# One weight load in five expert groups is cut by rows into transfers of 112, 8 and 8 rows

## The chip, the cores and the metric

The kernel runs on one core of a Trainium2 chip. A core has a matrix engine (TensorE, PE in the profile, with its weight loads as PEld), a vector engine (DVE), a scalar engine (ACT), GpSimd (POOL) and a sync engine (SP). SP issues nearly all transfers between the main memory and the on-chip memory; sixteen DMA engines carry them out. The on-chip memory has 128 rows (partitions). The metric is the device time of one execution in microseconds (us). Before the change it is 1357.66 us, the median of three runs from 1356.56 to 1358.91 us.

## What is computed

The reference is one decoder block on 256 tokens of width 2048: a norm, a token mixer (retention heads beside a state-space mixer, one input and one output projection), a norm, and a mixture of 32 experts in 4 groups with two experts chosen per token, then a final norm. The part that the change touches is the mixture of experts:

```
for grp in range(N_EXPERT_GROUPS):
    sl = slice(grp * EXPERTS_PER_GROUP, (grp + 1) * EXPERTS_PER_GROUP)
    a = jnp.einsum('td,edf->tef', ht, w_gate[sl])
    u = jnp.einsum('td,edf->tef', ht, w_up[sl])
    act = (jax.nn.silu(a.astype(f32)) * u.astype(f32) * comb[:, grp, :, None]).astype(h.dtype)
    out = out + jnp.einsum('tef,efd->td', act, w_down[sl]).astype(f32)
```

All three weight tensors of all 32 experts are read once: 32 x 3 x 2048 x 512 numbers of 4 bytes, 403 MB.

## The kernel before

The mixer comes first. Then the experts run in eight groups of four (`NG`, `GE`). The tokens that chose an expert of the group are gathered by matmuls with a 0/1 matrix (`gather`, tile `xg`, 32 places per expert). Three stages follow: the gate product (`project` into `pgate`), the up product (`project` into `pup`), and, after the product of the two, the down products with the scatter back to the tokens (`finish`, `back`).

The weights of a group lie in the main memory as 24 blocks of 128 rows by 4096 numbers, which are 16 KB a row and 2 MB a block. A block holds two tiles, each of which serves one step of 32-row matmuls for the four experts: blocks 0 to 7 are gate weights, 8 to 15 up weights, 16 to 23 down weights. The generator `stream` (line 762) takes the next buffer (`slot`, in the fixed order of `turns`, from rings of two to three buffers each and two halves of a larger tile named `twin`), issues one transfer on SP for the block (line 768), and hands out its two halves. In the last group alone the last two blocks go in two halves by columns.

What sets the order around the change is the program's own order and eight completion counters, which the transfers use in turn. A transfer waits on SP until the transfer eight places before it has landed, and until the matmuls that read the old content of its buffer are done. So at most eight transfers are under way. PE waits for a block's counter before the first matmul that reads it. `group` (line 1017) calls `stream` for one group. The last stage of the last group is followed by the final norm and the stores of the output.

Of the kernel before, what the change touches and what calls it, by code (L numbers as in the profile page):

```python
# [18 lines left out]
P = 128  # L19
# [14 lines left out]
NG = NE // GE  # L34
# [9 lines left out]
RING_A = 2  # L44
RINGS = {"a": RING_A, "b": 3, "e": 3, "n": 1}
SCRATCH = 256
PAD = 1.5e38


# [100 lines left out]
def block_kernel(tc, I, out):  # L150
    nc = tc.nc
    act, dve, pe, pool, sp = nc.scalar, nc.vector, nc.tensor, nc.gpsimd, nc.sync
# [6 lines left out]
    def stt(o, a, s, b, op0, op1, **k):  # L159
        dve.scalar_tensor_tensor(o, a, s, b, op0=op0, op1=op1, **k)  # L160

    def ts(o, a, s1, s2, op0, op1=None):
        if op1 is None:
            dve.tensor_scalar(o, a, s1, None, op0=op0)  # L164
        else:
            dve.tensor_scalar(o, a, s1, s2, op0=op0, op1=op1)
# [585 lines left out]
    def slot(n, name="wt"):  # L752
        if n in "cd":
            return twin("cd".index(n), 4).rearrange("p a b c -> p (a b) c")
        return rings[n].tile([P, 8, 512], F32, tag="w", name=name)
# [3 lines left out]
        sp.dma_start(w, src)  # L759
        return w  # L760

    def stream(src, n, single=0):

        for i in range(n // 2):
            w = slot(next(turns))
            s = src(i)
            for p in ((0, 4), (4, 8)) if i >= n // 2 - single else ((0, 8),):
                sp.dma_start(w[:, slice(*p)], s[:, slice(*p)])
            yield w[:, :4]
            yield w[:, 4:]  # L770

# [64 lines left out]
    lg = sm.tile([P, NT, 40], F32, name="lg")  # L836
    pool.memset(lg[:, :, :4], -PAD)
    mask = cp.tile([P, NT, NE], BF16, name="mask")
# [4 lines left out]
    def small(name, n):  # L843
        return sm.tile([P, NT, n], F32, name=name)


    gv, ev = small("gv", 15), small("ev", 14)
    pool.memset(gv[:, :, :7], -2 * PAD)
    pool.memset(ev[:, :, :6], -2 * PAD)
    mg, me = gv[:, :, 7:8], ev[:, :, 6:7]  # L850
# [4 lines left out]
    def b48(a):  # L855
        return a.unsqueeze(2).to_broadcast([P, 4, 8])
# [4 lines left out]
    def g48(a):  # L861
        return a.rearrange("p (g e) -> p g e", g=4)
# [11 lines left out]
    def route(t):  # L874
# [3 lines left out]
        dve.max(gv[:, t, 7:], lg[:, t, :8])  # L878
        dve.match_replace(gm[:, t], gv[:, t, :8], lg[:, t, :8], PAD)
        stt(mle[:, t], b48(gm[:, t, 4:]), PAD, g48(lg[:, t, 8:]), EQ, MUL)  # L880
        ts(g4[:, t], gm[:, t, 4:], PAD, None, EQ)
        dve.tensor_reduce(le[:, t], mle[:, t].rearrange("p g e -> p e g"), axis=AX, op=ADD)
# [132 lines left out]
        return nxt  # L1015

    def group(g):
        return stream(lambda i: I["wexp"][g, i], 48, 2 if g == NG - 1 else 0)


    xg = xgp.tile([P, KT, P], F32, name="xg")
    pgate = pbank("pg")
    ws = group(0)
    for k0, n in ((0, 1), (1, 1), *((k, 2) for k in range(2, KT, 2))):
        gather_part(xg, k0, n, (0, 1) if n == 1 else (1, 0))
# [81 lines left out]
    for g in range(NG):  # L1107
        if g:
            pgate = pbank("pg")
            ws = group(g)  # L1110
            project(pgate, xg, ((k, next(ws)) for k in range(KT)))
        if g + 1 < NG:
            e = slice(GE * g + GE, GE * g + 2 * GE)
            xg, swt = finish(xg, swt, pgate, ws, lambda: gather(posm[:, :, e], comb[:, :, e]), first=(g == 0))
        else:
            finish(xg, swt, pgate, ws, None, final_part)
# [5 lines left out]
    with tc.For_i(0, rounds, 1):  # L1122
        ts(posm, posm, -float(CAP), None, ADD)
        with tc.For_i(0, NG, 1) as gi:
            gd = bass.ds(gi, 1)
            ws = stream(lambda i: I["wexp"][gd, i].rearrange("a p e f -> p (a e) f"), 48)
            xg, swt = gather(posm[:, :, :GE], comb[:, :, :GE])
            pgate = pbank("pg")
            project(pgate, xg, ((k, next(ws)) for k in range(KT)))
            finish(xg, swt, pgate, ws)  # L1130
            for a in (posm, comb):
                tmp = ep.tile([P, NT, NE], F32, name="rot")
                dve.tensor_copy(tmp[:, :, :NE - GE], a[:, :, GE:])
                dve.tensor_copy(tmp[:, :, NE - GE:], a[:, :, :GE])
                dve.tensor_copy(a, tmp)
        for c0, n in ((0, 512), (512, 512), (1024, 512), (1536, P), (1664, P), (1792, P), (1920, P)):
            final_part(c0, n)
        final_norm()
# [19 lines left out]
```

## Time and profile before

| quantity | value |
|---|---|
| median of three runs | 1357.66 us (1356.56 to 1358.91) |
| profiled execution, its own time | 1354.11 us |
| its span, first to last instruction | 1352.3 us |
| mean granted share of PE's clock | 0.902 |
| PE busy | 1048.4 us (78%) |
| DVE busy | 401.3 us (30%) |
| ACT busy | 275.2 us (20%) |
| moved by the transfers | 487.03 MB, mean 360 GB/s |
| share of transfers in the chain that ended last | 61% |

The profile comes from one execution. Its span is cut into 40 slices of 33.8 us for the busy digits. The chain that ended last is followed back from the last instruction, at each step to what released it; a row "DMA" in it is the time from a transfer's issue to its landing. The DMA share is the mean busy share of the sixteen DMA engines in a stretch: at 0.5, half of their time is busy, be it half of the engines or all of them half of the time.

### The profile page before, as it was taken

Reading aid. Unit: us, or ns where it says so; the run is one execution under the profiler, and the core shown is the slowest. Engines: PE = TensorE matmul, PEld = TensorE weight load, DVE = VectorE, ACT = ScalarE, POOL = GpSimd, SP = SyncE. Lnnn points to the kernel's source line nnn. Section 1 sums busy time; section 2 is a strip of 40 time slices with the busy share of each in tenths; the row PEclk is TensorE's granted clock in tenths of the full one; section 3 lists DMA queues with packets and bytes.
Section 4 is the critical chain, followed back from the end, with each engine's and each line's share of the span. In section 5 each row is a group of like instructions: output and inputs, shape, how many; then the busy total and the mean of one; then the engine's idle time right before and its main releaser. Section 6 shows DMA issues by size and latency. Waiting matters only on the chain.

```text
span 1352.3 us, 17251 instructions
## 1 busy us (share of the span) xinstructions
PE 1048.4 (78%) x7319; PEld 597.4 (44%) x7319; DVE 401.3 (30%) x843; ACT 275.2 (20%) x512; POOL 6.7 (0%) x20
## 2 busy tenths in 40 slices
PE   9999999999999985587658557656855766585654
PEld 6999999888786441143114103211311321131112
DVE  6659878665556130021002002100200210020013
ACT  6655544555444000000000000000000000000003
POOL 0000000000000000000000000000000000000000
PEclk9999999999999998888789878977887997897888
DMA  9554555585976999999999999999999999999995
GB/s 376 213 179 145 206 209 203 187 324 188 404 274 227 383 426 427 428 426 425 427 428 429 426 426 427 427 427 427 426 427 427 429 426 426 427 428 427 426 426 217
DMA packets 38003, 487.03 MB, mean 360 GB/s; under 512 B 4481, under 2 KB 5153, under 8 KB 8353
## 3 DMA queue, kind: packets, MB, share of 16 engines
q1 hardware_dynamic: 37634, 485.58, 87.1%
q8 instruction: 59, 0.97, 0.3%
q10 hardware_dynamic: 288, 0.31, 0.1%
q14 instruction: 22, 0.18, 0.0%
HBM read 483.75 MB, written 2.11 MB: 359 GB/s over the span
## 4 chain that ended last, share of the span: by engine, by line
DMA 61%; PE 37%; DVE 0%; issue 0%; ACT 0%; SPq 0%; POOLq 0%; POOL 0%; DVEq 0%; ACTq 0%
DMA wt<-wexp 40%; DMA twin<-wexp 20%; PE pb L353 4%; PE pb L351 4%; PE pb L352 4%; PE pf L363 3%; PE pf L364 3%; PE pf L365 3%; PE po L723 2%; PE po L721 2%; PE po L722 2%; PE py L967 1%; PE pu L967 1%; PE pxg L941 1%; PE pg L967 1%; PE psc L998 1%
## 5 line engine op out<-in xcount | busy, mean ns | idle before, releaser
L967 PE MATMUL pu<-wt,xg 128*32 128x512 f32 x864 | 142.6, 789 | 97.6 <-DMA wt<-wexp 97.6
L967 PE MATMUL pg<-wt,xg 128*32 128x512 f32 x832 | 133.3, 769 | 87.8 <-DMA wt<-wexp 87.8
L157 DVE TENSOR_TENSOR wl<-w,wh 128x512 fp32r<-128x512 f32 x224 | 151.3, 689 | 72.6 <-ACT wh L285 71.8
L285 ACT ACTIVATE wh<-w 128x512 fp32r<-128x512 f32 x224 | 139.0, 630 | 138.2 <-PE pb L352 71.7
L157 DVE TENSOR_TENSOR sg<-sg,pu 128x512 f32<-128x512 f32 x8 | 5.5, 689 | 535.2 <-PE pu L967 534.1
L967 PE MATMUL py<-wt,at 128*32 128x128 f32 (+1 forms) x1456 | 115.7, 427 | 17.9 <-DMA wt<-wexp 17.7
L967 PEld LDWEIGHTS pu<-wt,xg 128*32 128x32 f32 x864 | 28.6, 128 | 208.3 <-DMA wt<-wexp 157.8
L967 PEld LDWEIGHTS pg<-wt,xg 128*32 128x32 f32 x832 | 25.3, 125 | 182.4 <-DMA wt<-wexp 137.8
L157 DVE TENSOR_TENSOR acc<-acc,psc 128x128 f32<-128x128 f32 (+1 forms) x98 | 43.3, 459 | 171.0 <-PE psc L998 170.9
L998 PE MATMUL psc<-y,swt 128*128 128x128 f32 (+1 forms) x224 | 72.7, 448 | 26.1 <-ACT y L995 25.5
L967 PEld LDWEIGHTS py<-wt,at 128*32 128x32 f32 x1456 | 42.5, 111 | 79.5 <-issue 37.8
L995 ACT ACTIVATE y<-py 128x128 f32<-128x128 f32 (+1 forms) x56 | 23.2, 415 | 233.9 <-PE py L967 233.8
L952 ACT ACTIVATE swt<-psw 128x256 f32<-128x256 f32 x8 | 3.1, 387 | 324.8 <-PE psw L950 324.8
L998 PEld LDWEIGHTS psc<-y,swt 128*128 128x128 f32 x224 | 33.8, 194 | 69.9 <-ACT y L995 57.7
L351 PE MATMUL pb<-xh,wh 128*128 128x256 f32 x224 | 64.3, 287 | 0.0
L941 PEld LDWEIGHTS pxg<-selr,h 128*128 128x128 f32 x512 | 61.2, 199 | 6.5 <-issue 5.9
L984 ACT ACTIVATE sg<-pg 128x512 f32<-128x512 f32 x8 | 4.8, 597 | 290.4 <-PE pg L967 290.4
L351 PE MATMUL pb<-twin,wh 128*128 128x256 f32 x224 | 63.8, 285 | 0.0
L941 PE MATMUL pxg<-selr,h 128*128 128x128 f32 x512 | 63.1, 284 | 0.6 <-DVE selr L164 0.6
L353 PE MATMUL pb<-xh,wl 128*128 128x256 f32 x224 | 63.4, 283 | 0.0
L352 PE MATMUL pb<-twin,wh 128*128 128x256 f32 x224 | 63.4, 283 | 0.0
L353 PE MATMUL pb<-twin,wl 128*128 128x256 f32 x224 | 63.4, 284 | 0.0
(256 smaller groups left out, 1449.2 us busy)
## 6 DMA issues: line engine op xcount, KB each, us to landing
wt<-wexp SPq DMA_DIRECT2D x156, 2048.0 KB, 39.1
twin<-wexp SPq DMA_DIRECT2D x34, 2048.0 KB, 39.1
w<-win SPq DMA_DIRECT2D x24, 2048.0 KB, 8.1
wt<-wout SPq DMA_DIRECT2D x6, 2048.0 KB, 12.4
w<-wout SPq DMA_DIRECT2D x2, 2048.0 KB, 7.9
wt<-wexp SPq DMA_DIRECT2D x4, 1024.0 KB, 31.9
w<-win SPq DMA_DIRECT2D x3, 1024.0 KB, 11.3
twin<-x SPq DMA_DIRECT2D x1, 2048.0 KB, 14.9
```

Of the source, the lines that this page charges most:

```text
L157: dve.tensor_tensor(o, a, b, op=op)
L285: act.activation(wh, w[:, i:i + n], AF.Copy)
L351: pe.matmul(o, wh[:, s], xh(k), start=(k == 0 and c % 2 == 0), stop=False, skip_group_check=True)
L352: pe.matmul(o, wh[:, s], xl(k), start=False, stop=False, skip_group_check=True)
L353: pe.matmul(o, wl[:, s], xh(k), start=False, stop=(k == KT - 1), skip_group_check=True)
L363: pe.matmul(ps[t], lh(k)[:, s], wh, start=(k == 0), stop=False)
L364: pe.matmul(ps[t], lh(k)[:, s], wl, start=False, stop=False)
L365: pe.matmul(ps[t], ll(k)[:, s], wh, start=False, stop=(k == KT - 1))
L721: pe.matmul(ps[t], yh[:, s], wh, start=(k == 0), stop=False)
L941: pe.matmul(px[:, i], h[:, t, (k0 + i) * P:(k0 + i + 1) * P], selr[:, t], start=(i == 0 and x == 0), stop=(x == NT - 1), skip_group_check= ...
L967: pe.matmul(ps[s], lhsT[:, s], w(j), **k)
L998: pe.matmul(px, swt[:, t * P:(t + 1) * P], y, start=True, stop=True)
```

## The change

In each of the groups 1 to 5, block 12 of the 24 (an up block) is moved in three transfers instead of one: rows 0 to 111, rows 112 to 119, and rows 120 to 127, all 4096 numbers wide. The bytes, the buffers and the order of the blocks stay. Nothing else is changed. The groups 0, 6 and 7 are loaded as before.

```
+APART_AT = 12
...
-    def stream(src, n, single=0):
+    def stream(src, n, single=0, apart=()):
 
         for i in range(n // 2):
             w = slot(next(turns))
             s = src(i)
             for p in ((0, 4), (4, 8)) if i >= n // 2 - single else ((0, 8),):
-                sp.dma_start(w[:, slice(*p)], s[:, slice(*p)])
+                for r in ((0, 112), (112, 120), (120, 128)) if i in apart else ((0, P),):
+                    sp.dma_start(w[slice(*r), slice(*p)], s[slice(*r), slice(*p)])
             yield w[:, :4]
             yield w[:, 4:]
...
     def group(g):
-        return stream(lambda i: I["wexp"][g, i], 48, 2 if g == NG - 1 else 0)
+        return stream(lambda i: I["wexp"][g, i], 48, 2 if g == NG - 1 else 0, (APART_AT,) if 0 < g < 6 else ())
```

The first place is SP's queue in group 1, around block 12. The names DMAHW0 to DMAHW7 are the eight completion counters, and PE_49 is PE's; the size is rows by numbers. Before:

```order
L768 DMA wt<-wexp 128x4096 [waits DMAHW0_49,PE_49]
L768 DMA wt<-wexp 128x4096 [waits DMAHW1_49,PE_49]
L768 DMA wt<-wexp 128x4096 [waits DMAHW2_49,PE_49]
L768 DMA twin_5187<-wexp 128x4096 [waits DMAHW3_49,PE_49]
L768 DMA wt<-wexp 128x4096 [waits DMAHW4_49,PE_49]
```

And with the change:

```order
L771 DMA wt<-wexp 128x4096 [waits DMAHW0_49,PE_49]
L771 DMA wt<-wexp 128x4096 [waits DMAHW1_49,PE_49]
L771 DMA wt<-wexp 112x4096 [waits DMAHW2_49,PE_49]
L771 DMA wt<-wexp 8x4096 [waits DMAHW3_49]
L771 DMA wt<-wexp 8x4096 [waits DMAHW4_49]
L771 DMA twin_5189<-wexp 128x4096 [waits DMAHW5_49,PE_49]
L771 DMA wt<-wexp 128x4096 [waits DMAHW6_49,PE_49]
```

The block takes three counters instead of one, so the blocks behind it use a counter two places further on; for the same counter, a block behind waits for a transfer that is now closer to it by two small ones.

The second place is PE's queue in the up product of group 1, where the same block is read. Before:

```order
L967 MATMUL pu<-wt,xg 32x512 [waits DMAHW1_49]
L967 MATMUL pu<-wt,xg 32x512 x7
L967 MATMUL pu<-wt,xg 32x512 [waits DMAHW2_49]
L967 MATMUL pu<-wt,xg 32x512 x7
L967 MATMUL pu<-twin_5187,xg 32x512 [waits DMAHW3_49]
```

And with the change:

```order
L970 MATMUL pu<-wt,xg 32x512 [waits DMAHW1_49]
L970 MATMUL pu<-wt,xg 32x512 x7
L970 MATMUL pu<-wt,xg 32x512 [waits DMAHW4_49,DMAHW3_49,DMAHW2_49]
L970 MATMUL pu<-wt,xg 32x512 x7
L970 MATMUL pu<-twin_5189,xg 32x512 [waits DMAHW5_49]
```

PE's instructions and their order are the same; the first matmul on the block waits for three landings instead of one.

## Rows read from the trace of the kernel before

**Rows 1.** The page's 40 slices: busy tenths of the DMA engines, and GB/s.
```profile
DMA  9554555585976999999999999999999999999995
GB/s 376 213 179 145 206 209 203 187 324 188 404 274 227 383 426 427 428 426 425 427 428 429 426 426 427 427 427 427 426 427 427 429 426 426 427 428 427 426 426 217
```
**Rows 2.** The chain that ended last, by engine.
```profile
DMA 61%; PE 37%; DVE 0%; issue 0%; ACT 0%; SPq 0%; POOLq 0%; POOL 0%; DVEq 0%; ACTq 0%
```
**Rows 3.** The same chain in order of time: start us, us, what.
```profile
496.37 39.15 DMA wt<-wexp
535.59 39.16 DMA twin<-wexp
574.80 39.14 DMA wt<-wexp
614.02 40.68 DMA wt<-wexp
...
811.60 40.63 DMA wt<-wexp
...
1009.15 40.66 DMA wt<-wexp
...
1216.47 40.64 DMA wt<-wexp
...
1295.09 33.21 DMA wt<-wexp
1328.43 0.81 PE py L967 x18
```
**Rows 4.** SP's own waits: us in total, times, longest us.
```profile
SPq L768 <- DMA wt<-wexp: 570.4, 133, 6.0
SPq L768 <- DMA twin<-wexp: 138.1, 31, 6.0
```
**Rows 5.** Busy time, 700 to 800: PE, PEld, DVE, ACT, POOL, clock, DMA share, GB/s.
```profile
700.00:800.00 100.00, 67.95 (x522) 26.20 (x514) 12.29 (x28) 3.89 (x9) 0.00 (x0) 0.86 1.01 427
```
**Rows 6.** Transfers from 500 to 1324 us, by queue and by issue.
```profile
q1 hardware_dynamic: 24206, 351.14, 100.4%
q8 instruction: 31, 0.51, 0.3%
...
wt<-wexp SPq DMA_DIRECT2D x131, 2048.0 KB, 39.1
```
**Rows 7.** End of the weights: stretch, us, PE's clock, DMA share, GB/s.
```profile
1326.00:1327.00 1.00, 1.00 0.97 401
1327.00:1328.00 1.00, 1.00 0.73 303
1328.00:1329.00 1.00, 1.00 0.61 254
1329.00:1330.00 1.00, 1.00 0.57 238
1330.00:1331.00 1.00, 1.00 0.51 213
1331.00:1332.00 1.00, 1.00 0.49 205
1332.00:1333.00 1.00, 1.00 0.49 205
1333.00:1334.00 1.00, 1.00 0.33 123
1334.00:1335.00 1.00, 1.00 0.20 82
1335.00:1336.00 1.00, 1.00 0.04 16
```
**Rows 8.** The issues of the weight transfers on SP: duration in ns min/median/max.
```profile
L768 SPq DMA_DIRECT2D wt<-wexp x160: 327/328/1184, 335.3 to 1306.2; - x160
```

More of the change, by code (lines that the diff above doesn't have):

```diff
@@ L46 @@
 SCRATCH = 256
+APART_AT = 12
 PAD = 1.5e38
@@ L760, in wload, with stream @@
         return w
-    def stream(src, n, single=0):
+    def stream(src, n, single=0, apart=()):
         for i in range(n // 2):
@@ L767, in stream @@
             for p in ((0, 4), (4, 8)) if i >= n // 2 - single else ((0, 8),):
-                sp.dma_start(w[:, slice(*p)], s[:, slice(*p)])
+                for r in ((0, 112), (112, 120), (120, 128)) if i in apart else ((0, P),):
+                    sp.dma_start(w[slice(*r), slice(*p)], s[slice(*r), slice(*p)])
             yield w[:, :4]
@@ L1017, in group @@
     def group(g):
-        return stream(lambda i: I["wexp"][g, i], 48, 2 if g == NG - 1 else 0)
+        return stream(lambda i: I["wexp"][g, i], 48, 2 if g == NG - 1 else 0, (APART_AT,) if 0 < g < 6 else ())
     xg = xgp.tile([P, KT, P], F32, name="xg")
```

## The prediction

> **What bounds the kernel now.** I read the 40 slices first, then the chain, then the waits of SP, and last the end of the weight stream in steps of 1 us. From about slice 14 on the transfers run at 426 to 429 GB/s without a gap to the last slice but one, and the busy digit stays at 9 [rows 1]. Transfers are 61% of the chain that ended last [rows 2]. PE is busy for 67.95 us of 100 in the middle of that stretch, with the DMA share at 1.01 [rows 5], so PE waits for weights there and not the other way round. SP waited 570.4 us + 138.1 us, nearly always on a transfer that had not landed [rows 4], and an issue takes 0.328 us [rows 8]: issuing is not the limit, the sixteen engines are. A block that lands later by 1 us in this stretch moves the end by 1 us: the chain goes from landing to landing, and the last landing that it needs is at 1295.09 + 33.21 = 1328.30 us, followed by a fixed tail of PE, ACT, DVE and stores [rows 3].
>
> Two numbers come from the chain. A plain step of eight blocks takes 39.14 us [rows 3], 4.89 us a block. A block has 128 rows over 16 engines, eight rows each, so a row of 16 KB takes 39.14 / 64 = 0.612 us on its engine. The second number: four of the steps take 40.63 to 40.68 us, 1.5 us more than the others [rows 3]. Four times 1.52 us is 6.1 us in which something holds up the slowest engine while others go on.
>
> The end of the stream shows who the others are. Engines run out of work one by one: the DMA share is 0.97 until 1327, 0.73 in the next step, then 0.51, and it stands at 0.49 from 1331 to 1333 before it falls to 0.04 [rows 7]. So eight engines end together at about 1328 and eight at about 1334. I call them the early and the late half. Taken exactly: the last early engine ends at about 1330.3 (the 0.51 of 1330 to 1331 is 0.02 x 16 = 0.3 us of one engine above eight), the last late one at about 1335.6 (0.04 x 16 = 0.6 us). The distance between the two is 5.3 us; between the middles of the halves (1327.8 and 1334.1, from adding up the shares on each side of one half) it is about 6.2 us, which agrees with the 6.1 us from the chain. The 31 packets of instructions in this stretch [rows 6] are a likely source of the hold-ups; the sum does not need it.
>
> **The change part by part.** *Issues.* Two more per split block, ten in all, 10 x 0.328 = 3.3 us on SP [rows 8]. They are hidden, since SP waits 5 us at nearly every block [rows 4]; without that cover it would be these 3.3 us. *Counters.* Of eight transfers under way, two are small while a split block is among them. With all three pieces among them, work for six blocks is queued instead of eight, 6 x 4.89 = 29 us. No engine is more than some 9 us ahead of another (1327 to 1336 [rows 7]), so none runs dry: nothing. *The wait of PE.* One wait on three landings instead of one: it ends with the last of the three, priced below.
>
> *Rows by engine.* The piece of 112 rows gives each of sixteen engines seven rows. A piece of eight rows, moved row by row, can employ at most eight engines, one row each. If both small pieces take the same eight engines, these get 7 + 2 = 9 rows, the other eight 7. Per split block that is +0.612 us for the one half and -0.612 us for the other, over five blocks 3.06 us each way. If the nine rows fall to the early half, the halves approach by 6.1 us, as much as they are apart.
>
> [...]
>
> *The pace of a row.* So far a row of a small piece is priced at 0.612 us. That price comes from transfers of 128 rows, in which every engine moves its own eight of the 128 rows, and all sixteen run at 427 GB/s side by side [rows 5]. Two things are new. Eight engines write eight neighbouring rows at the same time, rows that some other engines served in the blocks before; and with seven rows an engine, the 112 are dealt out along other borders. Whether neighbouring rows share a way in, no row of before shows. The bounds are these. From below: no sharing, 0.612 us. From above: the eight engines take turns through one way, 8 x 0.612 = 4.89 us for a small piece. I take the value half-way in doublings between one and eight, four at a turn with all eight at work in two sets: 4 x 0.612 = 2.45 us. For the 112 rows I take one row of seven that meets another engine, +0.612 us (from below 0; if every row met one, +4.28 us).
>
> [...]
>
> *Sum.* An engine of the half with the small pieces spends 7 x 0.612 + 0.612 + 2 x 2.45 = 9.8 us on a split block instead of 4.89: +4.9 us. Five blocks: +24.5 us. If it is the early half, 5.3 us are covered by its lead, and the end moves by 24.5 - 5.3 = +19.2 us. If it is the late half, nothing covers it: +24.5 us. I take the first. The profiled execution has 1354.1 us, so 1373.3 us. It lies 3.6 us under the median of the runs; on the median 1357.7 + 19.2 = 1376.9 us. The other bounds: two at a turn and no loss in the 112 rows give 4.28 + 2 x 1.22 - 4.89 = +1.83 us a block, 9.2 - 5.3 = +3.9 us, 1361.5 us. Eight at a turn give 4.28 + 9.78 - 4.89 = +9.2 us a block, 45.9 - 5.3 = +40.6 us, 1398 us.
>
> **Rivals.** *The balance* (faster). Rows take 0.612 us wherever they are written, and the small pieces fall to the early half. The late half ends 3.06 us sooner, at 1332.5, the early half 3.06 us later, at 1333.4; the end moves by 1335.6 - 1333.4 = 2.2 us, at best by the full 3.06. I take -2.5 us: 1355.2 us. For it: the five blocks shift just what the halves are apart, and no row shows a shared way in. Against: sixteen engines at full pace side by side say nothing of two on the same rows. *The wrong half* (slower). No sharing, but the small pieces fall to the late half. It gets five rows more, +3.06 us, 1360.7 us. For and against: no row tells the halves' numbers, and only one of two choices helps. *Nothing is shifted.* The eight rows are cut up and dealt to all sixteen engines, or alternate between the halves: each engine keeps eight rows' worth a block, and the time stays at 1357.7 us. Against it: rows went whole so far, 128 of 16 KB a block.
>
> **How the numbers follow.** Shared way in 0.56, balance 0.31, wrong half 0.07, nothing shifted 0.06. The likeliest case alone goes from 1361.5 to 1398 us. Since the balance holds more than 2 in 10, the range reaches down to it: 1354 to 1398 us. It leaves out the best ends of the balance and more than eight turns. A change of under 0.2% (2.7 us) is about what cannot be told from none here. The balance lies close to that bound: 0.18 of its 0.31 beyond it, 0.13 within. Of the shared way in 0.54 is slower and 0.02 within, of the wrong half 0.05 and 0.02, of nothing shifted 0.01 and 0.05. So faster 0.18, same 0.22, slower 0.60.
>
> **What would show it.** In the chain after, the steps that hold a split block should be some 5 us longer than 39.14 where I am right (less in the first ones, while the early half still has its lead), and the GB/s of that stretch should dip under 427 for some 10 us, with the engines still busy. If the balance is right, the steps stay at 39.14, the GB/s stay at 427 through all five, and at the end the share falls from 0.97 to near 0 in some 3 us, without the stand at 0.49. If the stand gets longer, the late half got the rows. A transfer of eight rows that lands as soon as its neighbours, or an end before 1354 us, would make the price of a row wrong; an end over 1398 us would mean that the 112 rows lose much more than I allow.

## The result, and the profile after

The changed kernel takes 1420.46 us, the median of six runs (1413.64 to 1426.44); the kernel before took 1357.11 us in six runs beside them (1355.25 to 1359.45). The ratio is 1.0463 (95% interval 1.0440 to 1.0486), 63 us slower. The forecast was +19.2 us and the range ended at 1398 us: the direction is right, the size is not. The profiled execution of the changed kernel has an own time of 1419.68 us, and its span is 1417.4 us.

The page's 40 slices of the changed kernel, busy tenths of the DMA engines and GB/s, answer to [rows 1]:

```profile
DMA  9445555666769999999999999999999999998993
GB/s 380 181 178 183 195 191 211 263 260 261 303 234 363 426 426 404 350 426 426 326 427 426 426 301 428 426 343 374 427 427 270 412 427 427 429 427 374 428 424 134
```

The engines are as busy as before, but the second row has five dips where [rows 1] had none: 404 and 350, 326, 301, 343 and 374, 270 and 412, one for each split block, each deeper than the first. (The 374 near the end is another matter, told below.) The engines are busy and move less, so their packets take longer: in the first dip a row of 16 KB took 1.09 to 1.28 us, and then up to 2.4, instead of 0.61 to 0.62 (below).

The chain that ended last, in order of time (start us, us, what), answers to [rows 3]:

```profile
633.19 39.13 DMA wt<-wexp
...
792.09 47.03 DMA wt<-wexp
839.18 34.88 DMA twin<-wexp
...
1358.91 34.79 DMA wt<-wexp
1393.83 0.82 PE py L970 x18
```

Plain steps still take 39.13 us. A step goes over eight transfers, though, and where small pieces are among the eight it holds fewer blocks than eight; so 34.88 is no gain, and 47.03 understates the loss. The last landing comes at 1358.91 + 34.79 = 1393.70 us, 65.4 us later than the 1328.30 of [rows 3], as much as the own time grew (1419.68 - 1354.11 = 65.6). A better ruler for where it went is from group to group. Of the kernel before, stretches between the starts of the product of gate and up on DVE, one a group: stretch, us, PE's clock, DMA share, GB/s. Each row ends with one of the groups 1 to 5:

```profile
475.00:587.90 112.90, 0.87 1.01 427
587.90:706.70 118.80, 0.82 1.01 427
706.70:824.80 118.10, 0.85 1.01 427
824.80:942.60 117.80, 0.86 1.01 427
942.60:1063.40 120.80, 0.84 1.01 427
```

And stretches of the changed kernel, the same columns: five of the same kind, then the first split block, the fifth, a stretch of the last group's gate weights, and the end of the weights:

```profile
475.10:597.70 122.60, 0.86 1.01 397
597.70:724.00 126.30, 0.80 1.01 398
724.00:856.60 132.60, 0.82 1.01 393
856.60:989.60 133.00, 0.79 1.01 391
989.60:1127.60 138.00, 0.76 1.01 383
...
562.00:566.00 4.00, 0.84 1.10 279
566.00:570.00 4.00, 0.58 0.96 217
570.00:574.00 4.00, 0.93 1.10 147
574.00:578.00 4.00, 0.50 0.89 184
578.00:582.00 4.00, 0.50 1.01 426
...
1060.00:1070.00 10.00, 0.50 1.01 429
1070.00:1080.00 10.00, 0.57 1.03 233
1080.00:1090.00 10.00, 0.60 1.00 211
1090.00:1095.00 5.00, 0.50 1.02 223
...
1296.00:1311.00 15.00, 0.73 0.75 301
...
1386.00:1388.00 2.00, 1.00 0.56 234
1388.00:1390.00 2.00, 1.00 0.16 66
1390.00:1395.00 5.00, 1.00 0.06 26
```

The five groups take 9.7, 7.5, 14.5, 15.2 and 17.2 us more than before: 64 us of the 65. Their lost throughput gives 53 us of it (122.6 x 30/427 = 8.6, then 8.6, 10.6, 11.2 and 14.2 us). That is the mean over the engines; the end goes by the slowest. The first dip lasts some 16 us, the fifth at least 25, and from 1095 to 1110 us the fifth is still at 334 and 374 GB/s.

The packets that the engines moved show the first dip from close by. A packet of the weights is one row of 16 KB; the others are 4 bytes long. Those that started from 565 to 570 us before, and from 565 to 570 and from 570 to 575 us in the changed kernel (packets, MB, share of sixteen engines' time):

```profile
q1 hardware_dynamic: 148, 2.16, 101.6%
```

```profile
q1 hardware_dynamic: 71, 1.08, 96.0%
```

```profile
q1 hardware_dynamic: 68, 0.75, 110.7%
```

In the trace of the kernel before, each of the 132 rows among them took 0.61 to 0.62 us. In the changed kernel all 66 rows of the first 5 us took 1.09 to 1.28 us, and of the 46 rows of the next 5 us 22 took 2.0 to 2.4 us and none under 1.28. So every row that started there was slowed, first to about twice its time. In the later dips more rows are slow, but not slower: 35 of the 191 rows that took over 0.7 us in the first dip took over 1.6, and 8 of 438 in the fifth.

At the end, instead of two halves that stop 5.3 us apart [rows 7], most engines stop by 1390 and a share of 0.06, one engine of sixteen, is left after that.

The stretch from 1296 us is of the same kind. There SP holds the stream back for one early load of the final norm's weights, in both kernels for about as long. Its waits in the kernel before, then in the changed one (us in total, times, longest):

```profile
SPq L1068 <- DMA twin<-wexp: 20.7, 1, 20.7
```

```profile
SPq L1071 <- DMA twin<-wexp: 19.2, 1, 19.2
```

Before, the transfers under way covered it; [rows 1] has no dip there. Now the DMA share falls to 0.75: a quarter of the engines' time is idle while the others still work off what is queued, as it would be if the engines had run apart. The end does not pay for this dip, since the stretch from 1127.60 us to the last instruction takes 289.8 us, against 288.9 us before (1417.4 less 1127.60; 1352.3 less 1063.40).

SP's waits grew and its issues did not: it waited 630.0 us on the first kind of landing instead of 570.4 us [rows 4], at 0.328 us an issue as in [rows 8].

### The profile page after: what moved, and what is told of

It is laid out like the page before. It is cut to its first block, busy times and chain, and to the rows that moved or that the text cites. A ratio compares the mean times of both kernels' runs of the same rounds, so it can differ in the third digit from the quotient of the medians.

```text
span 1417.4 us, 17266 instructions
## 1 busy us (share of the span) xinstructions
PE 1059.6 (75%) x7319; PEld 598.4 (42%) x7319; DVE 401.3 (28%) x843; ACT 275.1 (19%) x512; POOL 6.7 (0%) x20
## 2 busy tenths in 40 slices
DMA packets 38083, 487.03 MB, mean 344 GB/s; under 512 B 4561, under 2 KB 5233, under 8 KB 8433
## 4 chain that ended last, share of the span: by engine, by line
DMA 66%; PE 32%; DVE 0%; issue 0%; SPq 0%; ACT 0%; POOLq 0%; POOL 0%; DVEq 0%; ACTq 0%
DMA wt<-wexp 42%; DMA twin<-wexp 24%; PE pb L355 4%; PE pb L353 4%; PE pb L354 4%; PE pf L365 3%; PE pf L366 3%; PE pf L367 3%; PE po L725 2%; PE po L723 2%; PE po L724 2%; PE pg L970 1%; DMA w<-win 1%; PE pxg L944 1%; PE pyd L532 0%; PE psc L576 0%
## 5 line engine op out<-in xcount | busy, mean ns | idle before, releaser
L970 PE MATMUL pu<-wt,xg 128*32 128x512 f32 x864 | 154.3, 846 | 152.0 <-DMA wt<-wexp 152.0
L970 PE MATMUL py<-wt,at 128*32 128x128 f32 (+1 forms) x1456 | 115.3, 426 | 17.9 <-DMA wt<-wexp 17.2
L970 PEld LDWEIGHTS py<-wt,at 128*32 128x32 f32 x1456 | 42.3, 110 | 78.1 <-issue 40.6
L354 PE MATMUL pb<-xl,wh 128*128 128x256 f32 x224 | 63.1, 282 | 0.0
```

The lines of the kernel that those rows point to most:

```text
L354: pe.matmul(o, wh[:, s], xl(k), start=False, stop=False, skip_group_check=True)
L970: pe.matmul(ps[s], lhsT[:, s], w(j), **k)
```

## The experiments

Theory A was that rows on the chip share ways in, so that a transfer over other rows than all 128 slows the engines. Against it stood the number of transfers with their counters (B), and the small pieces alone (C). Edits are shown against the changed kernel; +us is the median less that of the kernel before, run beside it.

**Three pieces by columns.** All 128 rows in each, as many transfers and counters as in the change.

```diff
-                for r in ((0, 112), (112, 120), (120, 128)) if i in apart else ((0, P),):
-                    sp.dma_start(w[slice(*r), slice(*p)], s[slice(*r), slice(*p)])
+                for c in ((p[0], 6), (6, 7), (7, p[1])) if i in apart else (p,):
+                    sp.dma_start(w[:, slice(*c)], s[:, slice(*c)])
```

> The same five blocks go in three transfers by columns (3072, 512 and 512 numbers wide), all of 128 rows. Theory A, a shared way in by row number: every engine keeps its own eight rows, so nothing changes, within 3 us of before. Theory B, the number of transfers or the counters cost: the same ten transfers more as in the changed kernel, so some +60 us. Theory C, transfers of eight rows on eight engines cost: no change either.

1355.84 us against 1355.69: ratio 1.0001 (0.9991 to 1.0011). The stretch with the first such block (columns as above):

```profile
555.00:575.00 20.00, 0.74 1.02 426
```

No dip. Ten more transfers and their counters cost nothing, so B is out. (PE's wait is not quite the same here: the first half of the block lies wholly in the first piece.)

**Two pieces, 112 and 16 rows.**

```diff
-                for r in ((0, 112), (112, 120), (120, 128)) if i in apart else ((0, P),):
+                for r in ((0, 112), (112, 128)) if i in apart else ((0, P),):
```

> 112 rows and 16 rows, both on sixteen engines. Theory A: seven rows at about two engines a way in (7 x 1.22 us) and one row at four (2.45 us) against 4.89 us: +6.1 us a block, +31 us or more in all. Theory C (only the eight-row pieces on eight engines cost, as the prediction had it): at most +0.6 us a block from the 112 rows and +1.8 us from the 16 rows, so up to +12 us. Theory B: half of the added transfers, some +30 us.

1399.53 us, ratio 1.0326 (1.0290 to 1.0362), +44. The stretch of the first split block:

```profile
564.00:568.00 4.00, 0.50 1.09 320
568.00:572.00 4.00, 0.50 1.00 221
572.00:576.00 4.00, 0.70 1.06 176
```

Without any piece of eight rows 44 of the 63 us remain, so the eight-row pieces are not the whole. The pace falls to about half (221 of 427 GB/s) ahead of its slowest 4 us (176), by the order of issue already in the first, large piece.

**Two halves of 64 rows.**

```diff
+                for r in ((0, 64), (64, 128)) if i in apart else ((0, P),):
```

> Two transfers of 64 rows, both on sixteen engines, four rows each. Theory A: 64 rows reach half of the ways in, two engines on each, 1.22 us a row: 9.8 us a block instead of 4.89, +4.9 us, +24 us in all, and some 213 GB/s while the block moves. Theory C: no change. Theory B: as the kernel with 112 and 16 rows.

1399.12 us, ratio 1.0323 (1.0280 to 1.0366), +43.

```profile
568.00:572.00 4.00, 0.50 0.97 209
572.00:576.00 4.00, 0.50 0.96 205
```

The pace is 205 to 209 GB/s of 427, a half, where theory A expected some 213. The loss at the end, 43 us, was larger than the 24 us of five blocks at half the pace: the stream is slow for longer than the block alone would need.

**Eight pieces of 16 rows: neighbours, and every eighth.** The second edit lets each piece take every eighth row.

```diff
+                for r in tuple((16 * j, 16 * j + 16) for j in range(8)) if i in apart else ((0, P),):
...
+                for r in tuple((j, P, 8) for j in range(8)) if i in apart else ((0, P),):
```

> Eight transfers of 16 neighbouring rows, each on sixteen engines, one row each. Theory A: sixteen engines on four ways in, four at a turn, 8 x 2.45 = 19.6 us a block instead of 4.89, +14.7 us, +73 us in all, and some 107 GB/s while the block moves. Theory C: no change. Theory B: seven transfers more a block instead of two, 3.5 times the loss of the changed kernel, some +220 us.

> Eight transfers of 16 rows again, but each takes every eighth row of the block, in the memory and on the chip. Theory A, a shared way in by on-chip row number: sixteen rows eight apart reach eight ways in instead of four, two engines on each: half of the pace (some 213 GB/s) while the block moves, and less loss than with 16 neighbouring rows (+52 us). Theory M, neighbouring rows in the main memory collide: hardly a loss, since rows eight apart are 128 KB apart. Theory S, a transfer that has not all 128 rows is slow for itself: as with 16 neighbouring rows, +52 us.

Neighbours: 1407.80 us, ratio 1.0387 (1.0317 to 1.0457), +52. Every eighth: 1395.01 us, ratio 1.0280 (1.0251 to 1.0310), +38. The slowest 5 us of the first such block, neighbours first:

```profile
565.00:570.00 5.00, 0.50 1.04 157
```

```profile
565.00:570.00 5.00, 0.50 0.95 197
```

The order is as A has it, though 157 is above the pace I had expected. The two runs with neighbours lie 16 us apart (1399.99 and 1415.62), so the times alone would not carry the difference.

**Which end of the transfer.** In these two the block lies in the main memory in another order of rows. In the first the pieces are every eighth row on the chip and 16 neighbours in memory; in the second `src` and `dst` are exchanged.

```diff
+    for g in range(1, 6):
+        b = o["wexp"][g, APART_AT].copy()
+        for r, q in zip(dst, src):
+            o["wexp"][g, APART_AT, slice(*q)] = b[slice(*r)]
...
+                for r, q in zip(dst, src) if i in apart else (((0, P), (0, P)),):
+                    sp.dma_start(w[slice(*r), slice(*p)], s[slice(*q), slice(*p)])
```

> The on-chip side of the run before (every eighth row), but the rows of each transfer lie side by side in the main memory (the five blocks are laid out so). Theory A: as the run before, since only the on-chip rows count. Theory M: as with 16 neighbouring rows, +52 us and some 150 GB/s.

> The other way round: 16 neighbouring rows on the chip, every eighth row in the main memory. Theory A: as with 16 neighbouring rows on both sides, +52 us and some 150 GB/s while the block moves. Theory M: hardly a loss.

Every eighth on the chip: 1396.99 us, ratio 1.0295 (1.0240 to 1.0350), +40. Neighbours on the chip: 1409.43 us, ratio 1.0387 (1.0334 to 1.0440), +53. The slowest 5 us again, in that order:

```profile
565.00:570.00 5.00, 0.76 1.06 226
```

```profile
570.00:575.00 5.00, 0.50 0.94 138
```

Both times go with the rows on the chip and not with those in memory (38 and 40 us against 52 and 53), and so do the single rows of 16 KB: those that started from 565 to 575 us took 1.23 and 1.25 us in the median with every eighth row on the chip, and 1.69 and 1.80 us with 16 neighbours. So what slows a row is decided on the chip's side; a way in that engines share there is theory A's picture of it, which no run shows directly.

**One split block alone, early and late.** First group 1 only, then group 5 only.

```diff
+        return stream(..., (APART_AT,) if g == 1 else ())
...
+        return stream(..., (APART_AT,) if g == 5 else ())
```

> The change of the kernel (112, 8 and 8 rows) in group 1 alone. If every split block costs the same: a fifth of +63 us, +12.7 us. If the first costs less because the engines are still close together and the later ones more because each split leaves them further apart: some +5 to +8 us.

> The change (112, 8 and 8 rows) in group 5 alone, the place of the block that cost +17.3 us in the changed kernel. Theory H, a split block costs more the further the splits before it have driven the engines apart: without them it costs about as much as in group 1 alone, +4 to +8 us. Theory T, it costs more the later it comes, because the late half falls back by itself: some +15 us.

Early: 1361.48 us, ratio 1.0043 (1.0023 to 1.0064), +4.9. Late: 1366.48 us, ratio 1.0090 (1.0054 to 1.0126), +12.2. The dip of the early one, then of the late one:

```profile
560.00:564.00 4.00, 1.00 1.09 356
564.00:568.00 4.00, 0.63 1.01 229
568.00:572.00 4.00, 0.50 1.17 193
572.00:576.00 4.00, 0.50 0.81 147
576.00:580.00 4.00, 0.50 0.97 377
```

```profile
1030.00:1035.00 5.00, 0.50 1.10 360
1035.00:1040.00 5.00, 0.71 1.00 206
1040.00:1045.00 5.00, 0.64 1.08 200
1045.00:1050.00 5.00, 0.68 0.90 174
1050.00:1055.00 5.00, 0.66 0.98 279
```

By the medians the same block costs over twice as much late as early, with no other split before it. The intervals of the two losses just overlap (3.1 to 8.7 us, and 7.3 to 17.1), but the late dip is longer as well. The early dip lacks 4 x (71 + 198 + 234 + 280 + 50) / 427 = 7.8 us of work, the late one 5 x (67 + 221 + 227 + 253 + 148) / 427 = 10.7 us. So by the medians about 3 us of the early one were covered at the end, and nothing of the late one; within the intervals the early one may also have been covered not at all.

**Five split blocks in a row in group 1.** Is it the time in the stream that makes a late block dear, or the splits before it?

```diff
+        return stream(..., tuple(range(8, 13)) if g == 1 else ())
```

> Five split blocks as in the change, but one behind the other (blocks 8 to 12 of group 1). Theory H: the engines are driven apart all the same, so some +50 to +70 us. Theory T: the late half is hardly behind in group 1, so five times the cost of one block there, +25 us.

1390.50 us, ratio 1.0268 (1.0238 to 1.0298), +36, 7.2 us a block. That lies between the two expectations: neither holds as it stands, and since splits that follow each other at once share one slow stretch (a block takes 4.89 us, the dip of one alone some 16 us), the run does not divide the growth between them.

**Eight-row pieces, spread and side by side.** Four pieces of eight rows and one of 96: every fourth row, then eight neighbours.

```diff
+                for r in tuple((j, 32, 4) for j in range(4)) + ((32, 128),) if i in apart else ((0, P),):
...
+                for r in tuple((8 * j, 8 * j + 8) for j in range(4)) + ((32, 128),) if i in apart else ((0, P),):
```

> Rows 0 to 31 in four transfers of eight rows, each taking every fourth row, and rows 32 to 127 in one. By theory A the eight engines of a small piece then write eight different ways in. So they keep 0.61 us a row, and all the loss comes from the piece of 96 rows. Theory E, a transfer on eight engines is slow for itself: as the next run, with neighbouring rows.

> The same numbers of transfers, engines and rows as the run before, but each small piece takes eight neighbouring rows. Theory A: four engines on a way in, up to 2.45 us a row, four pieces a block: up to 4 x 1.83 = 7.3 us a block more than the run before, some +37 us over five blocks, less where other engines hide it. Theory E: no difference to the run before.

Spread: 1408.56 us, ratio 1.0401 (1.0371 to 1.0431), +54. Neighbours: 1422.29 us, ratio 1.0502 (1.0472 to 1.0533), +68. That neighbouring rows cost more is as A has it, but the difference is 13.7 us, 2.7 us a block, well under what I expected. Most of the 68 us is there with the spread pieces, which by theory A have ways of their own. Theory A gives those 54 us to the 96-row piece; that a transfer on eight engines costs something for itself is not excluded as a part of them.

**All engines brought to a common start.** Theory D: a split block costs more as the engines drift apart. In the first kernel nothing is split, but ahead of block 12 of the five groups the weight stream runs empty (round trips of four numbers a row, which transfers around it wait for). The second does the same and splits the block as the change does.

```diff
+    gone = calm_dram.tile([P, 4], F32, name="gone")
...
+            if i in calm:
+                sp.dma_start(gone, w[:, 0, :4])
             w = slot(next(turns))
+            if i - 3 in calm or i - 2 in calm or i - 1 in calm or i in calm:
+                sp.dma_start(w[:, 0, :4], gone)
+            if i in calm:
+                for _ in range(3):
+                    sp.dma_start(gone, w[:, 0, :4])
+                    sp.dma_start(w[:, 0, :4], gone)
```

> No block is split. Ahead of block 12 of groups 1 to 5, SP makes four round trips of 16 bytes a row between the chip and the main memory, each waiting for the one before, so that the transfers under way run out and all engines start block 12 together. It is the kernel to hold the next run against; the round trips themselves cost some 5 to 20 us a group.

> The same round trips, and block 12 of groups 1 to 5 in 112, 8 and 8 rows. Theory D, what a split costs grows with the distance between the engines: after a common start every split costs no more than the one in group 1 alone, so 15 to 30 us more than the run before (3 to 6 us a block), and no growth from group to group. If the distance has nothing to do with it: some +60 us, as in the changed kernel.

1409.80 us (ratio 1.0399, 1.0353 to 1.0446) without the split, 1438.46 us (1.0611, 1.0568 to 1.0653) with it: 28.7 us for five split blocks, 5.7 us each, where the change pays 63. From group to group the second takes 4.1, 5.4, 4.4, 6.9 and 6.5 us more than the first: little growth. Its fifth split block:

```profile
1135.00:1140.00 5.00, 0.50 0.64 182
1140.00:1145.00 5.00, 0.50 1.08 390
1145.00:1150.00 5.00, 0.50 1.10 272
1150.00:1155.00 5.00, 0.50 0.86 121
```

The stream did run empty, at 1 GB/s from 1130 to 1135 us. The slow stretch after the start-up is 10 us (272 and 121 GB/s), where the changed kernel's fifth has 25 at least. The rows of 16 KB say the same for all five blocks: what they took beyond 0.615 us, over sixteen engines, comes to 5.5, 6.2, 6.5, 5.7 and 5.9 us in the slow stretches here, and to 8.4, 8.6, 10.6, 11.6 and 14.4 us in the changed kernel. The drain also empties the queues, so the runs show that a common start takes the extra cost away, not that the distance between engines is the only thing it resets.

**112 and 16 rows in group 1 alone.**

```diff
+                for r in ((0, 112), (112, 128)) if i in apart else ((0, P),):
...
+        return stream(..., (APART_AT,) if g == 1 else ())
```

> 112 and 16 rows in group 1 alone. By the way-in theory the 16 rows take four engines a way in for one row (2.45 us), the two pieces of eight rows take that twice: so some 2.4 us less than with 112, 8 and 8 rows in group 1 alone (+4.9 us), +2 to +3 us.

1361.93 us, ratio 1.0047 (1.0024 to 1.0070), +5.3, as much as with two pieces of eight (+4.9). I expected less, and missed. The runs of each kernel lie 3 to 4 us apart, so the 2.4 us that I expected between the two do not show, and are not excluded either.

No version that beats the kernel before came out of this: the cut by columns is its equal, and every cut by rows is slower.

## Why the prediction was right or wrong

**The bound, the issues, the counters: right.** The DMA engines set the end (transfers are 61% of the chain before and 66% after), and the issues and counters that were priced at nothing cost nothing (1.0001 with the cut by columns). The dips under 427 GB/s with busy engines came as the prediction said they would, but lasted 16 us and more instead of some 10.

**The shared way in: right as far as the runs go.** The loss is decided by the rows on the chip: with the memory's rows exchanged, the times stay (+38 and +40 us with every eighth row, +52 and +53 with neighbours), and so does the time of a row (1.23 and 1.25 us, 1.69 and 1.80). The way itself stays an explanation of these numbers. Balance, wrong half and nothing shifted all had rows at 0.612 us wherever they are written, and fall with it.

**The 112 rows: the step that failed.** I took one row of seven that meets another engine, +0.612 us. The first dip shows 217 GB/s in the part that goes, by the order of issue, with the 112 rows, half of 427, each row there takes 1.09 to 1.28 us instead of 0.612, and 112 + 16 rows lose 5.3 us in group 1 and 44 us in five groups without any eight-row piece. That is close to the bound that I wrote down and did not use, every row meeting another engine, +4.28 us a block. I had argued that the 112 are dealt out along other borders, which no row shows, and let one collision stand for it. With the +4.28 us in place of the 0.612, my sum per block is 4.9 + 3.7 = 8.6 us; the early dip lacks 7.8 us. Five such blocks less the lead give 5 x 8.6 - 5.3 = 37.7 us, 1395 us. The range failed on the same term: its end, 1398 us, was worked out with no loss in the 112 rows at all, and the prediction had named an end beyond it as the sign that these rows lose much more than it allows.

**The small pieces: near the price of a row, their share of the end not settled.** I put 2.45 us on a row, a choice between two bounds with no row of before behind it. In the last part of the first dip 22 of 46 rows took 2.0 to 2.4 us; the trace does not mark which of them belong to the small pieces. That such a piece employs eight engines and the 112 rows sixteen agrees with the packets of 4 bytes: the changed kernel has 80 packets under 512 B more than the kernel before (4561 against 4481), 5 x (16 + 8 + 8 - 16), and the cut by columns, with ten more transfers of all 128 rows, 160 more (4641). That both small pieces take the same eight engines, the 2 x 2.45 us of my sum, was my assumption and no run shows it. What a second small piece adds to the end does not come out the same twice: nothing that shows in group 1 alone (4.9 against 5.3 us), but 63 against 44 us over five blocks.

**The lead of 5.3 us: partly right.** By the medians about 3 us of one early block's 7.8 were covered (7.8 less 4.9), and nothing late.

**Five blocks at one price: wrong, and the other step that failed.** I multiplied by five. Alone, the block costs 4.9 us in group 1 and 12.2 us in group 5 by the medians; in the change the groups lose 9.7, 7.5, 14.5, 15.2 and 17.2 us. Brought to a common start they cost 5.7 us each, 28.7 us together. The difference of 34 us between 28.7 and 63 is a cost that my sum had no term for. I had the sign of it in hand: the steps of 40.6 us [rows 3] and the halves that end 5.3 us apart [rows 7] say that engines drift, and I counted the drift as a lead to be used up, not as something that makes the next collision longer. That it is the drift, and not something else that the drain resets, is argued and not shown.

**What stays open.** Why every row that started in the first dip was slowed, whichever engine moves it; which engine gets which rows, of a whole block or of the 112, and which half got the small pieces, since no row carries engine numbers (so whether the early half was the right choice stays unknown); how many engines a transfer of 16 or 64 rows employs, for which the expectations have sixteen; and how the growth divides between time in the stream and earlier splits.

## What to carry to other kernels

Where a stream of transfers is the bound, cut a load by columns and keep all 128 rows in each piece: that was free here (ratio 1.0001), and a block cut by rows into 112, 8 and 8 cost 5 to 17 us. Do not price a disturbance of such a stream once and multiply: look whether the engines run apart from each other, and try the last place as well as the first. Do not price the rows of a piece by those of whole blocks: here a row went from 0.61 us to 1.09 to 1.28 us in the first dip, and five cut blocks cost 63 us.

## What the runs showed of the hardware

A transfer over seven eighths of the rows slowed the whole stream to about half its pace (217 of 427 GB/s) with all sixteen engines shown busy (a share of 0.96), and each row of 16 KB to 1.09 to 1.28 us from 0.61; transfers over 64 rows slowed it as much (205 to 209). Pieces of every eighth row went at 197 and 226 GB/s in their slowest 5 us, pieces of 16 neighbouring rows at 157 and 138, whichever rows of the memory they came from. One split block cost 4.9 us (3.1 to 8.7) at 560 us into the program and 12.2 us (7.3 to 17.1) at 1030 us, and 5.7 us on the mean of five places after the engines had started together.
